# Two-layer mLSTM and retention trunk: head 1's first z column under the gate chain, a reordered start, masks made ahead, the state's low part on VectorE

## The chip, the cores and the metric

The kernel runs on one core of one Trainium2 chip. The metric is the device time of one execution in microseconds (us), as the median of several executions. The engines are named as in the profile: PE is TensorE, DVE is VectorE, ACT is ScalarE, POOL is GpSimd, and SP is the engine whose queue issues all DMA transfers here.

## The reference

Two layers run one after the other on x (1024 tokens by 1024 channels, float32). Each layer does this:

```python
ada = silu(c) @ w_ada[l] + b_ada[l]            # 3072 values: shift, scale, gate
h = rmsnorm(x, norm_g[l]) * (1 + scale) + shift
p = h @ w_in[l]                                # 9224 columns, split among the heads
# 4 mLSTM heads of 256: q and k through a causal convolution over 4 tokens and SiLU; v; o; z;
#   one input and one forget gate value per token and head; a stabilised chunked recurrence
y_m = sigmoid(o) * layernorm(cell) * silu(z)
# 4 retention heads of 256: q and k turned by rotary angles, v, z; decay gamma_h per token
y_r = layernorm(ret) * silu(z)
x = x + gate * (concat(y_m, y_r) @ w_out[l])
```

A last RMSNorm follows the second layer. Everything is float32, and the result is held to float32 accuracy.

## The kernel before

**Products.** A float32 product is made of three fast ones: each operand is split into a high part (a cast on ACT, to the fp32r type) and a low part (the difference, a tensor_tensor on DVE or POOL, in `split_to`), and `mm3` issues high by high, high by low and low by high (lines 134 to 136). The normalised input stands transposed in `hT`, 8 blocks of 128 channels by 2 halves of 512 tokens, each with both parts.

**Units and ticks.** PE's instructions stand in the order in which the program emits them. The projection of 128 columns of `w_in` is four units (`proj_units`): two halves of the tokens, each half in two units of 12 products. After every unit comes a tick. Side work is written as generators that are launched with a delay: at each tick those that are due run to their next yield, and what they emit stands at that place in PE's order. The instructions of the other engines are ordered by a scheduler within their dependences; each engine then runs its own list strictly in order, and so does SP's queue, which carries every DMA.

**The start (layer 0).** A script of short steps orders the work by hand: T transposes a block of x on PE, E scales and shifts it, C and U make its two parts, F multiplies it into the first three weight columns, A adds up rows of `w_ada` on DVE, P and G make scale and shift of two blocks from such a sum, W splits weights, N, Q, R and X normalise rows. `w_ada` is loaded in quarters (`ada_load`), x in halves (`load_x`). DMA transfers of the start are issued in program order: x's first half, the small rows, the first `w_ada` quarter, three weight blocks, the second quarter, and so on.

**The gate chain.** `v0_units` makes head 0's v and the gate values of all heads. `gate_chain` turns the gate values into running sums and maxima per token (scans on DVE, 4 partitions by 512), stores the maxima to DRAM (`mdr`), and 15 ticks after its launch PE transposes its tables (line 492). In layer 0 these ticks are the units of head 0's o column (4), its q columns (8) and 3 units of its k columns.

**Heads.** For each head 0 to 7: gate columns z and o (`gate_path`, z alone for retention heads), q and k (with the convolution on DVE for mLSTM heads, lines 613 to 621), v, then `attention` is launched and runs under the next head's projections. It works on 4 chunks of 256 tokens: `scores` (products of k and q, times a mask), `values` (scores by v, plus the state by q), `update` (the state, in `cf`, split into `cH` by ACT and `cL` by POOL), `finish` (to DRAM). An mLSTM head's mask `dm` is made in `scores`: two transfers from `mdr`, two affine_selects on POOL, two exponentials on ACT. There are two `dm` buffers, and the scheduler already places the mask work of a later chunk, or of the next head, as soon as a buffer is free.

**Other side work in layer 0.** `rotary_tables` is launched after head 1 and computes the angles on DVE. `ada_columns_later` is launched after head 2: it reads layer 1's `w_ada` rows through the four `raw` buffers that the weights use too, and adds them up on DVE (line 255). `gate_rows` is launched after head 5 and does the same for the output gate.

Of the kernel before, what the change touches and what calls it, by code (L numbers as in the profile page):

```python
# [69 lines left out]
def tile_hybrid_trunk(ctx, tc, x, c, positions, w_ada, b_ada, norm_g, w_in, conv_w, conv_b,  # L70
# [285 lines left out]
    def rotary_tables():  # L356
        c1, c2, c3 = two_pi_split()
        tiles = [wt("g", 512, 6) for _ in range(3)]
        ang, turn, tmp, rnd, a1, pos = (t[:, i * CH:(i + 1) * CH] for t in tiles for i in range(2))
        a2 = ang  # L360
        for n in range(4):
            i, cs = n // 2, slice((n % 2) * CH, (n % 2 + 1) * CH)
            Q.dma_start(pos.bitcast(I32), positions[0:1, n * CH:(n + 1) * CH].to_broadcast([P, CH]))
            yield 2
            V.tensor_copy(ang, pos.bitcast(I32))
            V.tensor_scalar(ang, ang, kc[:, C_FREQ:C_FREQ + 1], None, ALU.mult)
            V.tensor_copy(a1.bitcast(F32R), ang)
            yield 1
            V.tensor_tensor(a2, ang, a1, ALU.subtract)
            V.tensor_scalar(turn, a1, c3, None, ALU.mult)  # L370
            yield 1
            V.scalar_tensor_tensor(turn, a2, c3, turn, ALU.mult, ALU.add)
            V.scalar_tensor_tensor(turn, a2, c2, turn, ALU.mult, ALU.add)
            yield 1
            for src, cc in ((a1, c2), (a2, c1), (a1, c1)):
                V.tensor_scalar(tmp, src, cc, None, ALU.mult)
                V.tensor_scalar(rnd, tmp, MAG_I, -MAG_I, ALU.add, ALU.add)
                yield 1
                V.tensor_tensor(tmp, tmp, rnd, ALU.subtract)
                V.tensor_tensor(turn, turn, tmp, ALU.add)  # L380
                yield 1
            for which, sh in ((1, 0.0), (0, 0.25)):
                if sh:
                    V.tensor_scalar(turn, turn, sh, None, ALU.add)
                V.tensor_scalar(rnd, turn, MAG_I, -MAG_I, ALU.add, ALU.add)
                V.tensor_tensor(tmp, turn, rnd, ALU.subtract)
                yield 1
                V.tensor_scalar(tmp, tmp, 0.49999994, -0.49999994, ALU.min, ALU.max)
                Q.dma_start(rdr[which][i][:, cs], tmp)
                yield 2  # L390

    def v0_gates(l):
        gr = wt("wgr", KT * 8, 1)
# [151 lines left out]
    def ocol(hg, m):  # L545
        return OFF_MO + hg * HD + m * P

    def gate_path(l, hg, hT, res, m0=0, m1=2):
        for m in range(m0, m1):
            w = load_w(w_in[l], zcol(hg, m), P)  # L550
            yield from proj_units(w, hT, z_evac(res, m, None if hg < 4 else gdr[l][hg]))
            if hg < 4:
                w = load_w(w_in[l], ocol(hg, m), P)
                yield from proj_units(w, hT, o_evac(res, m, gdr[l][hg]))
# [165 lines left out]
    def attention(l, hg, gt, qT, kT, kt, vs, gp, rot):  # L720
# [3 lines left out]
        nrm = [None] * NCH  # L724
        st = {"state": None, "cf": None}

        def scores(j):
            half, jo = j // 2, (j % 2) * CH
            if ml:
                dm = wt("dm", 512, 2)[:, 0:384]  # L730
                Q.dma_start(dm[:, 0:256], mdr[l][h:h + 1, j * CH:(j + 1) * CH].to_broadcast([P, CH]))
                Q.dma_start(dm[:, 256:384], mdr[l][h:h + 1, j * CH + P:(j + 1) * CH].to_broadcast([P, P]))
                G.affine_select(dm[:, 0:256], dm[:, 0:256], [[1, 256]], ALU.is_ge, BIG, base=0, channel_multiplier=-1)
                G.affine_select(dm[:, 256:384], dm[:, 256:384], [[1, 128]], ALU.is_ge, BIG, base=0, channel_multiplier=-1)
                for tt, sl in ((0, slice(0, 256)), (1, slice(256, 384))):
                    A.activation(dm[:, sl], dm[:, sl], AF.Exp, scale=-1.0, bias=gt["C4"][:, 2 * j + tt, 0, h:h + 1])
                dmat = dm
            else:
                dmat = rmask
            ps = ps_a()  # L740
            pd = ps[:, CH:2 * CH].rearrange("p (a b) -> p a b", a=2)
            for dt in range(2):
                kk, qq = kT[dt][half], qT[dt][j]
                ks = slice(jo, jo + P)
                mm3(ps[:, 0:CH], (kk[0][:, ks], kk[1][:, ks]), (qq[:, 0:CH], qq[:, CH:2 * CH]), dt == 0, dt == 1)
            for dt in range(2):
                kk = kT[dt][half]
                qd = qT[dt][j].rearrange("p (a b) -> p a b", a=2)[:, :, P:CH]
                for i in range(2):
                    PE.matmul(pd, kk[i][:, jo + P:jo + CH], qd, start=dt == 0 and i == 0, stop=dt == 1 and i == 1)  # L750
            sd = wt("th", 512, 5)
            V.tensor_tensor(sd[:, 0:CH], ps[:, 0:CH], dmat[:, 0:CH], ALU.mult)
            V.tensor_tensor(sd[:, CH:2 * CH].rearrange("p (a b) -> p a b", a=2), pd,
                            dmat[:, CH:CH + P].unsqueeze(1).to_broadcast([P, 2, P]), ALU.mult)
            V.tensor_tensor(sd[:, CH:CH + P], sd[:, CH:CH + P], sd[:, CH + P:2 * CH], ALU.add)
            sd = sd[:, 0:CH + P]
            sH, sL = wt("sH", 384, 2, F32R), wt("sL", 384, 2, F32R)
            split_to((sH, sL), sd)
            sds[j] = (sH, sL)

        def update(j):
            if j == 0:
# [4 lines left out]
            for dt in range(2):  # L767
# [7 lines left out]
                else:  # L775
                    dec = gt["dc"][:, h, j - 1:j] if ml else float(np.float32(GAMMA[h] ** CH))
                    V.scalar_tensor_tensor(cf[:, dt, 0:W], cf[:, dt, 0:W], dec, pu[:, 0:W], ALU.mult, ALU.add)
            split_to((new[0][:, :, 0:W], new[1][:, :, 0:W]), cf[:, :, 0:W])
            st["state"] = new

        def values(j):
# [59 lines left out]
        def finish(j):  # L841
# [10 lines left out]
            if hg == 3 and j == NCH - 1:  # L852
                with tc.issue_after(last.ins):
                    load_rotary(rot)

        scores(0)
        yield 1
        scores(1)
        yield 2 if hg == 0 else 1
        for j in range(NCH):  # L860
            values(j)
            yield 1
            if j < NCH - 1:
                update(j)
            yield 1
            if j + 2 < NCH:
                scores(j + 2)
            if hg != 3:
                yield 1
            finish(j)  # L870
            yield 1
# [146 lines left out]
    xss = [new_ss(), new_ss()]  # L1018
    crow = wt("rows", P, 2)
    Q.dma_start(crow[0:8, :], c[0].rearrange("(r c) -> r c", c=P))  # L1020
    xts = [load_x(0)]
    arows = load_ada_rows(0)
    araw = [ada_load(0, 0)]
    firsts = (zcol(0, 0), ocol(0, 0), zcol(0, 1))
    rw = [[w_raw(col, 0)] for col in firsts]
    araw.append(ada_load(0, 1))
# [7 lines left out]
    hrows = load_head_rows(0)  # L1034

    load_cact(crow)
    squares(xts[0], xss[0], range(4), (1, 3))
    accs = [bt()]
    ada_cols(0, arows)
    rs0 = row_rstd(xss[0], "nrm")  # L1040
    ada_group(araw[0], accs[0], range(3))
    norm_scale(xts[0], rs0, (0,), (0, 2))
    ada_group(araw[0], accs[0], range(3, 8))
    pad = ps_a()

    for l in range(DEPTH):
# [14 lines left out]
        if l == 0:  # L1061
            seq = [(half, k) for half in range(2) for k in range(4)]
            seq += [(half, k) for g in (2, 3) for half in range(2) for k in (2 * g, 2 * g + 1)]
            w0, pts, hfs, rs1 = [], {}, {}, []
            script = ("T0 P0 T1 W00 W10 N G0 E0 C0 E1 C1 A102 U0 U1 W20 F0 F1 T2 A126 Q04 A168 P1 G1 E2 C2 R X0 T3 E3 C3 "
# [4 lines left out]
            for step in script.split():  # L1070
# [2 lines left out]
                if what == "T":  # L1073
                    pts[n] = norm_transpose(xts[seq[n][0]], seq[n][1])
                elif what == "E":
                    hfs[n] = norm_evac(0, pts.pop(n), seq[n][1], True)
                elif what == "C":
                    half, k = seq[n]
                    hT[k][half] = (bt(F32R), bt(F32R))
# [16 lines left out]
                    squares(xts[1], xss[1], range(int(arg[0]), int(arg[1])))  # L1096
                elif what == "R":
                    rs1 = row_rstd(xss[1], "nrm")
                elif what == "N":
                    norm_scale(xts[0], rs0, (1,), range(4))  # L1100
                elif what == "X":
                    if n == 0:
                        norm_scale(xts[1], rs1, (0,))
# [5 lines left out]
                        vrw.append(v0_raw(0, n + 4))  # L1109
                else:  # L1110
                    i, p = (int(d) for d in arg)
                    wf[i] += split_w(rw[i][p], P, V)
            head_cols(0, hrows)
            startup.__exit__(None, None, None)
        else:
# [18 lines left out]
        else:  # L1134
            run_units(proj_units(load_w(w_in[l], zcol(0, 1), P), hT, z_evac(gp, 1)))
        run_units(proj_units(load_w(w_in[l], ocol(0, 1), P), hT, o_evac(gp, 1, gdr[l][0])))
        gb = []
        for hg in range(8):
            ml = hg < 4
            if hg == 0:  # L1140
                rot = [[], []]
            if hg > 0:
                gp = [[None, None], [None, None]]
                run_units(gate_path(l, hg, hT, gp, 0, 1 if hg == 7 else 2))
            vs = []
            kt = [None] * NCH
            kT = [[None, None], [None, None]]
# [3 lines left out]
            for which, res in ((0, qT), (1, kT)):  # L1151
                if ml:
                    run_units(qk_ml(l, hg, which, hT, gt, kt, res))
                else:
                    run_units(qk_ret(l, hg % 4, which, hT, kt, res, *rot))
            if hg not in (0, 4):
                run_units(v_path(l, hg, hT, gt, vs))
            if hg == 0:
                launch(v0_splits(gt, vraw, vs), 1)
            launch(attention(l, hg, gt, qT, kT, kt, vs, gp, rot), 4 if hg == 0 else 0)  # L1160
            if hg == 7:
                loads = OutLoads(l)
                loads.stage(2)
# [3 lines left out]
                launch(rotary_tables(), 0)  # L1167
            if hg == 5:
                launch(gate_rows(l, gb))
            if hg == 2 and l + 1 < DEPTH:  # L1170
                launch(ada_columns_later(l + 1))
        nhT = [[None, None] for _ in range(KT)]
        if l == DEPTH - 1:
# [50 lines left out]
```

## Time and profile before

| what | value |
| --- | --- |
| median of 3 executions | 2345.45 us (2345.41 to 2346.18) |
| the profiled execution's own time | 2349.28 us |
| its span, first to last instruction | 2347.6 us |
| mean granted TensorE clock | 0.994 |
| PE busy | 2297.6 us, 98% of the span |
| DVE, ACT, POOL busy | 1283.7, 895.4, 883.8 us |

A window row gives the length of a stretch, then busy us (and number of instructions) of PE, its weight loads, DVE, ACT and POOL, then the granted clock, the share of the DMA engines and GB/s. A wait row gives who waited for whom, total us, how often, and the longest. A timeline row gives start, duration, engine, line, operation, tiles, and in brackets the idle time before it and what ended it. A group row gives busy us, mean ns of one, and the idle time before.

### The profile page before, as it was taken

How to read it: one execution, taken by the hardware profiler on the slowest of the kernel's cores; microseconds unless marked ns; L12 is line 12 of the kernel's file. 1: busy time of each engine (PE TensorE's matmuls, PEld its weight loads, DVE VectorE, ACT ScalarE, POOL GpSimd, SP SyncE). 2: the span in 40 equal slices, each digit the busy share in tenths (PEclk: the TensorE clock that was granted, in tenths of full speed). 3: DMA queues.
4: the chain of work that ended last, by engine and by line, in shares of the span. 5: the costliest groups of instructions: out<-in, count | busy, mean ns of one | idle time of the engine just before them, and what ended most of it. 6: DMA issues, size and time to landing. Idle time of an engine off the chain costs nothing.

```text
span 2347.6 us, 34389 instructions
## 1 busy us (share of the span) xinstructions
PE 2297.6 (98%) x12589; PEld 1980.6 (84%) x12589; DVE 1283.7 (55%) x2694; ACT 895.4 (38%) x1744; POOL 883.8 (38%) x846
## 2 busy tenths in 40 slices
PE   6989999999999999999999999999999999999998
PEld 4878888889988988988888888888898888988886
DVE  7375587655554544475525655455543445456753
ACT  6535343434332323343434444343433322324442
POOL 0344343433344334323453444343333434451313
PEclk9999999999999999999999999999999999999999
DMA  8323232433432424377422323323323323424872
GB/s 253 79 68 86 73 88 72 114 95 105 135 91 72 121 69 113 86 242 255 167 80 76 83 72 78 80 68 81 81 71 81 81 78 103 134 76 157 265 229 81
DMA packets 326970, 260.50 MB, mean 111 GB/s; under 512 B 75892, under 2 KB 262012, under 8 KB 326800
## 3 DMA queue, kind: packets, MB, share of 16 engines
q1 hardware_dynamic: 326800, 258.30, 38.9%
q8 instruction: 99, 1.62, 0.3%
q14 instruction: 71, 0.58, 0.1%
HBM read 202.61 MB, written 55.61 MB: 110 GB/s over the span
## 4 chain that ended last, share of the span: by engine, by line
PE 88%; DVE 4%; DMA 3%; issue 2%; POOL 1%; ACT 1%; SPq 1%; POOLq 0%; ACTq 0%; DVEq 0%
PE pp L134 23%; PE pp L135 23%; PE pp L136 23%; PE pa L136 6%; PE pa L135 6%; PE pa L134 6%; PE pa L750 1%; DMA b<-in_w_ada_dram 1%; DMA b<-in_x_dram 0%; DVE acc L616 0%; POOL b L599 0%; DMA g<-gdr 0%; DMA dm<-mdr 0%; PE pa L304 0%; DMA raw<-in_w_in_dram 0%
## 5 line engine op out<-in xcount | busy, mean ns | idle before, releaser
L134 PE MATMUL pp<-b,wH 128*128 128x512 f32 x1776 | 704.9, 397 | 1.3 <-ACT b L1080 1.3
L135 PE MATMUL pp<-b,wH 128*128 128x512 f32 x1776 | 702.2, 395 | 0.0
L136 PE MATMUL pp<-b,wL 128*128 128x512 f32 x1776 | 702.0, 395 | 0.0
L599 POOL TENSOR_TENSOR wL<-raw,wH 128x512 fp32r<-128x512 f32 x338 | 449.0, 1335 | 582.3 <-ACT wH L598 518.3
L136 PEld LDWEIGHTS pp<-b,wL 128*128 128x128 f32 x1776 | 334.9, 189 | 79.3
L134 PEld LDWEIGHTS pp<-b,wH 128*128 128x128 f32 x1776 | 335.6, 189 | 72.1 <-ACT b L1080 1.7
L135 PEld LDWEIGHTS pp<-b,wH 128*128 128x128 f32 x1776 | 335.3, 189 | 71.2 <-DVE b L1083 0.6
L598 ACT CAST wH<-raw 128x512 fp32r<-128x512 f32 x402 | 247.0, 617 | 377.0 <-PE pp L136 124.8
L136 PE MATMUL pp<-wH,b 128*128 128x256 f32 (+1 forms) x1152 | 353.0, 306 | 2.5 <-DVE b L894 2.5
L134 PE MATMUL pp<-wH,b 128*128 128x256 f32 (+1 forms) x1152 | 353.3, 307 | 0.0
L135 PE MATMUL pp<-wL,b 128*128 128x256 f32 (+1 forms) x1152 | 352.9, 306 | 0.0
L599 POOL TENSOR_TENSOR b<-acc,b 128x256 fp32r<-128x256 f32 (+1 forms) x208 | 200.4, 983 | 316.4 <-ACT b L598 305.1
L136 PEld LDWEIGHTS pp<-wH,b 128*128 128x128 f32 x1152 | 216.7, 188 | 14.7 <-DVE b L894 3.4
L135 PEld LDWEIGHTS pp<-wL,b 128*128 128x128 f32 x1152 | 216.9, 188 | 10.6
L134 PEld LDWEIGHTS pp<-wH,b 128*128 128x128 f32 x1152 | 216.6, 188 | 10.6
L598 ACT CAST b<-acc 128x256 fp32r<-128x256 f32 (+1 forms) x208 | 93.6, 487 | 198.2 <-DVE acc L693 135.8
L616 DVE SCALAR_TENSOR_TENSOR acc<-pp,cols,acc 128x511 f32<-128x511 f32 (+2 forms) x192 | 142.5, 742 | 47.3 <-ACT acc L611 45.2
L599 POOL TENSOR_TENSOR sL<-th,sH 128x384 fp32r<-128x384 f32 x64 | 70.6, 1103 | 154.5 <-ACT sH L598 127.4
L134 PE MATMUL pa<-wH,b 128*128 128x512 f32 x256 | 101.0, 395 | 0.0
L135 PE MATMUL pa<-wL,b 128*128 128x512 f32 x256 | 100.8, 394 | 0.0
L136 PE MATMUL pa<-wH,b 128*128 128x512 f32 x256 | 100.7, 393 | 0.0
L620 ACT ACTIVATE th<-acc 128x512 f32<-128x512 f32 x64 | 40.4, 632 | 149.8 <-DVE acc L618 77.2
(249 smaller groups left out, 3485.1 us busy)
## 6 DMA issues: line engine op xcount, KB each, us to landing
raw<-in_w_in_dram SPq DMA_DIRECT2D x274, 256.0 KB
raw<-in_w_out_dram SPq DMA_DIRECT2D x128, 256.0 KB
gdr<-g SPq DMA_DIRECT2D x64, 256.0 KB
ndr<-zt SPq DMA_DIRECT2D x128, 128.0 KB
raw<-in_w_ada_dram SPq DMA_DIRECT2D x64, 256.0 KB
g<-ndr SPq DMA_DIRECT2D x64, 256.0 KB
g<-gdr SPq DMA_DIRECT2D x64, 256.0 KB
acc<-kdr SPq DMA_DIRECT2D x192, 64.0 KB
```

The lines of the kernel that those rows point to most:

```text
L134: PE.matmul(o, lt[0], rt[0], start=start, stop=False)
L135: PE.matmul(o, lt[0], rt[1], start=False, stop=False)
L136: PE.matmul(o, lt[1], rt[0], start=False, stop=stop)
L598: A.copy(dst[0], src)
L599: eng.tensor_tensor(dst[1], src, f(dst[0]), ALU.subtract)
L616: V.scalar_tensor_tensor(acc[:, d:], pt[:, 0:HALF - d], wcol, acc[:, d:], ALU.mult, ALU.add)
L620: A.activation(th, acc, AF.Tanh, scale=0.5)
L750: PE.matmul(pd, kk[i][:, jo + P:jo + CH], qd, start=dt == 0 and i == 0, stop=dt == 1 and i == 1)
```

## The change

1. **z column.** In layer 0 the projection of head 1's first z column (`zcol(1, 0)`) is emitted right after head 0's last o column, so that its four units stand among the 15 ticks before the gate chain's transposes. Head 1's `gate_path` leaves it out.
2. **Start.** The first `w_ada` quarter is loaded ahead of x's first half. Its sum is made first, then x is squared and normalised (new steps S and N0 in the script). The first two blocks are scaled on DVE instead of ACT, and the low parts of the first three weight blocks move from DVE to POOL.
3. **Masks.** `scores` is divided: `dm_load` issues the transfers (the first two at the start of `attention`, the later ones at the end of `scores(j)` for chunk j+2) and `dm_make` the affine_selects and exponentials (for chunk j+2 after `values(j)`). For heads 1 to 3 `attention` is launched before the v projection with a delay of 7, and head 0's delay falls from 4 to 2, so that the scores stand at the tick at which they stood.
4. **State.** The state's low part `cL` is made on DVE instead of POOL, for all heads of both layers.
5. **Side work.** `ada_columns_later` is launched after head 3 instead of head 2. `rotary_tables` writes its sine and cosine into two buffers and issues both transfers together.

```diff
-            for which, sh in ((1, 0.0), (0, 0.25)):
+            parts = ((1, 0.0, tmp), (0, 0.25, a1))
+            for which, sh, dst in parts:
...
+            for which, sh, dst in parts:
+                Q.dma_start(rdr[which][i][:, cs], dst)
+            yield 2
...
-    def gate_path(l, hg, hT, res, m0=0, m1=2):
+    def gate_path(l, hg, hT, res, m0=0, m1=2, z0=True):
...
+            if m or z0:
+                w = load_w(w_in[l], zcol(hg, m), P)
...
+        def dm_load(j):
+            if ml and j < NCH:
+                dm = dms[j] = wt("dm", 512, 2)[:, 0:384]
...
+        def dm_make(j):
+            if ml and j < NCH:
+                dm = dms[j]
...
             split_to((sH, sL), sd)
             sds[j] = (sH, sL)
+            dm_load(j + 2)
...
-            split_to((new[0][:, :, 0:W], new[1][:, :, 0:W]), cf[:, :, 0:W])
+            split_to((new[0][:, :, 0:W], new[1][:, :, 0:W]), cf[:, :, 0:W], V)
...
+        if ml:
+            dm_load(0)
+            dm_load(1)
+            yield 1
+            dm_make(0)
+            dm_make(1)
+            yield 1
         scores(0)
...
             values(j)
             yield 1
+            dm_make(j + 2)
...
-    xts = [load_x(0)]
     arows = load_ada_rows(0)
     araw = [ada_load(0, 0)]
+    xts = [load_x(0)]
...
-    squares(xts[0], xss[0], range(4), (1, 3))
+    ada_cols(0, arows)
     accs = [bt()]
-    ada_cols(0, arows)
-    rs0 = row_rstd(xss[0], "nrm")
-    ada_group(araw[0], accs[0], range(3))
-    norm_scale(xts[0], rs0, (0,), (0, 2))
-    ada_group(araw[0], accs[0], range(3, 8))
+    ada_group(araw[0], accs[0], range(KT))
...
-            script = ("T0 P0 T1 W00 W10 N G0 E0 C0 E1 C1 A102 U0 U1 W20 F0 F1 T2 A126 Q04 A168 P1 G1 E2 C2 R X0 T3 E3 C3 "
+            script = ("P0 G0 S N0 T0 T1 W00 W10 E0 E1 C0 C1 U0 U1 W20 F0 F1 N1 T2 A103 Q04 A136 A168 P1 G1 E2 C2 R X0 T3 E3 C3 "
...
-                    hfs[n] = norm_evac(0, pts.pop(n), seq[n][1], True)
+                    hfs[n] = norm_evac(0, pts.pop(n), seq[n][1], n >= 2)
...
-                    wf[i] += split_w(rw[i][p], P, V)
+                    wf[i] += split_w(rw[i][p], P, V if p else G)
...
+        gp1 = [[None, None], [None, None]]
+        if l == 0:
+            run_units(proj_units(load_w(w_in[l], zcol(1, 0), P), hT, z_evac(gp1, 0)))
...
+            if 0 < hg < 4:
+                launch(attention(l, hg, gt, qT, kT, kt, vs, gp, rot), 7)
...
-            launch(attention(l, hg, gt, qT, kT, kt, vs, gp, rot), 4 if hg == 0 else 0)
+            if hg == 0 or hg > 3:
+                launch(attention(l, hg, gt, qT, kT, kt, vs, gp, rot), 2 if hg == 0 else 0)
...
-            if hg == 2 and l + 1 < DEPTH:
+            if hg == 3 and l + 1 < DEPTH:
                 launch(ada_columns_later(l + 1))
```

More of the change, by code (lines that the diff above doesn't have):

```diff
@@ L385, in rotary_tables @@
                 V.tensor_scalar(rnd, turn, MAG_I, -MAG_I, ALU.add, ALU.add)
-                V.tensor_tensor(tmp, turn, rnd, ALU.subtract)
+                V.tensor_tensor(dst, turn, rnd, ALU.subtract)
                 yield 1
-                V.tensor_scalar(tmp, tmp, 0.49999994, -0.49999994, ALU.min, ALU.max)
-                Q.dma_start(rdr[which][i][:, cs], tmp)
-                yield 2
+                V.tensor_scalar(dst, dst, 0.49999994, -0.49999994, ALU.min, ALU.max)
+            yield 2
+            for which, sh, dst in parts:
+                Q.dma_start(rdr[which][i][:, cs], dst)
+            yield 2
     def v0_gates(l):
@@ L546, in ocol @@
         return OFF_MO + hg * HD + m * P
-    def gate_path(l, hg, hT, res, m0=0, m1=2):
+    def gate_path(l, hg, hT, res, m0=0, m1=2, z0=True):
         for m in range(m0, m1):
-            w = load_w(w_in[l], zcol(hg, m), P)
-            yield from proj_units(w, hT, z_evac(res, m, None if hg < 4 else gdr[l][hg]))
+            if m or z0:
+                w = load_w(w_in[l], zcol(hg, m), P)
+                yield from proj_units(w, hT, z_evac(res, m, None if hg < 4 else gdr[l][hg]))
             if hg < 4:
@@ L725, in attention @@
         st = {"state": None, "cf": None}
[L727 to L730, printed above, removed]
+        dms = {}
+        def dm_load(j):
+            if ml and j < NCH:
+                dm = dms[j] = wt("dm", 512, 2)[:, 0:384]
                 Q.dma_start(dm[:, 0:256], mdr[l][h:h + 1, j * CH:(j + 1) * CH].to_broadcast([P, CH]))
                 Q.dma_start(dm[:, 256:384], mdr[l][h:h + 1, j * CH + P:(j + 1) * CH].to_broadcast([P, P]))
+        def dm_make(j):
+            if ml and j < NCH:
+                dm = dms[j]
                 G.affine_select(dm[:, 0:256], dm[:, 0:256], [[1, 256]], ALU.is_ge, BIG, base=0, channel_multiplier=-1)
@@ L736, in scores @@
                     A.activation(dm[:, sl], dm[:, sl], AF.Exp, scale=-1.0, bias=gt["C4"][:, 2 * j + tt, 0, h:h + 1])
-                dmat = dm
-            else:
-                dmat = rmask
+        def scores(j):
+            half, jo = j // 2, (j % 2) * CH
+            dmat = dms.pop(j) if ml else rmask
             ps = ps_a()
@@ L1098, in tile_hybrid_trunk @@
                     rs1 = row_rstd(xss[1], "nrm")
+                elif what == "S":
+                    squares(xts[0], xss[0], range(4), (1, 3))
+                    rs0 = row_rstd(xss[0], "nrm")
                 elif what == "N":
-                    norm_scale(xts[0], rs0, (1,), range(4))
+                    norm_scale(xts[0], rs0, (n,), range(4) if n else (0, 2))
                 elif what == "X":
@@ L1142, in tile_hybrid_trunk @@
             if hg > 0:
-                gp = [[None, None], [None, None]]
-                run_units(gate_path(l, hg, hT, gp, 0, 1 if hg == 7 else 2))
+                gp = gp1 if hg == 1 else [[None, None], [None, None]]
+                run_units(gate_path(l, hg, hT, gp, 0, 1 if hg == 7 else 2, hg > 1 or l > 0))
             vs = []
```

## The prediction

> **What bounds the kernel now.** I read the page's busy shares first, then PE's waits over the whole run, then windows laid around each wait, then the timeline inside them. On the page PE is the bound:
>
> ```profile
> PE 2297.6 (98%) x12589; PEld 1980.6 (84%) x12589; DVE 1283.7 (55%) x2694; ACT 895.4 (38%) x1744; POOL 883.8 (38%) x846
> ```
>
> The change adds and removes no product, so it can win only PE's idle time, 2347.6 - 2297.6 = 50.0 us, and what PE loses at a low clock after a pause. PE's waits, longest totals of interest, with count and longest:
>
> ```profile
> PE pa L492 <- DVE b L482: 7.0, 1, 7.0
> ...
> PE pa L134 <- ACT nd L796: 4.9, 2, 3.4
> ...
> PE pa L135 <- POOL cL L599: 1.6, 2, 1.2
> ...
> PE pa L136 <- POOL sL L599: 1.3, 2, 0.6
> ```
>
> The windows around them: length, then busy us of PE, its loads, DVE, ACT, POOL, and the granted clock.
>
> ```profile
> 98.40:141.20 42.80, 42.79 (x187) 34.45 (x186) 34.52 (x50) 21.32 (x32) 14.71 (x15) 1.00 0.25 60
> 141.20:148.20 7.00, 0.00 (x0) 0.00 (x0) 6.81 (x12) 2.02 (x4) 2.32 (x2) 0.85 0.05 1
> 148.20:153.00 4.80, 4.76 (x14) 3.91 (x15) 4.77 (x18) 3.72 (x11) 2.69 (x3) 0.50 0.31 37
> ...
> 326.00:329.50 3.50, 1.40 (x9) 0.82 (x7) 2.92 (x7) 2.83 (x7) 1.58 (x2) 1.00 0.32 115
> ...
> 354.80:357.50 2.70, 1.25 (x5) 0.57 (x5) 2.70 (x6) 1.62 (x3) 1.66 (x2) 1.00 0.29 84
> ...
> 458.10:464.50 6.40, 2.97 (x15) 2.12 (x13) 0.43 (x2) 1.77 (x5) 1.07 (x3) 0.93 0.58 168
> 464.50:470.00 5.50, 5.50 (x19) 4.93 (x20) 3.25 (x15) 1.68 (x4) 1.59 (x2) 0.50 0.19 48
> 560.00:625.00 65.00, 63.93 (x444) 59.17 (x443) 36.09 (x107) 24.14 (x53) 23.82 (x23) 1.00 0.34 96
> 1295.00:1480.00 185.00, 184.36 (x998) 158.47 (x997) 107.28 (x258) 86.04 (x178) 78.17 (x81) 1.00 0.31 78
> ```
>
> The reader should see two large holes, at the gate chain (141.2) and under head 3's gate columns (458.1), each followed by a stretch at half clock. The last row is layer 1's first heads, without rotary tables and without `w_ada` rows under them: 0.64 us idle in 185 us. What is lost in layer 0 is therefore lost to side work, which the change moves.
>
> **z column under the gate chain.** PE waits 7.00 us at line 492 and then runs 4.80 us at 0.50 of its clock, which costs another 4.80 x 0.50 = 2.40 us: 9.4 us in all. The Trainium skill, "TensorE: Matmul & The Clock Gate" (What's actually happening), has the array at half rate until one busy window of about 3.4 us has passed, which would be 1.7 us instead of 2.40 and would make the final sum 0.7 us later.
>
> PE reaches the transposes after 15 units in both kernels, so 141.2 stays. What must come earlier is DVE's line 482. Between 122.68, when the first half column of q is through, and 148.10 DVE also did the following convolution work (three answers of the windows view, restricted to lines 616, 618 and 621 in this order), and the gate chain ended behind it:
>
> ```profile
> 122.68:148.10 25.42, 6.55 (x9) 0.96 0.21 50
> 122.68:148.10 25.42, 3.23 (x5) 0.96 0.21 50
> 122.68:148.10 25.42, 1.39 (x3) 0.96 0.21 50
> ...
> 147.41 0.69 DVE L482 TENSOR_TENSOR b<-b,b 4x512 f32<-4x512 f32 x1
> ...
> L528 DVE SCALAR_TENSOR_TENSOR g<-th,pp 128x512 f32<-128x512 f32 x62 | 42.0, 677 | 49.1 <-ACT th L526 49.1
> ```
>
> That is 11.17 us. In the changed order of DVE's instructions only one of these (the first line 616 of the second half column, 6.55 / 9 = 0.73) still stands ahead of the chain's last instruction; two z evacuations at 0.68 come in instead. So the chain ends 11.17 - 0.73 - 1.36 = 9.1 us earlier, at 148.1 - 9.1 = 139.0, against 141.2. The wait goes with 2.2 us to spare, and the half clock with it: -9.4 (bounds -9.4 and -4.7, if half of the work stays ahead). What is late next is head 0's mask and decay tables, which now have four units more before they are needed. The z transfers and the weights of that column pass no queue they did not use before. Head 0's attention, on the other hand, now runs under 12 gate units and then q's convolutions, where it had 16: I take +0.5, between 0 and +1.3, the total of the sL waits quoted above.
>
> **`w_ada` rows moved from head 2 to head 3.** The hole at 458.1:
>
> ```profile
> 452.14 2.78 DVE L255 SCALAR_TENSOR_TENSOR b<-raw,cact,b 128x512 f32<-128x512 f32 x2 [0.62 <-DMA raw<-in_w_ada_dram]
> ...
> 455.18 0.41 DVE L753 TENSOR_TENSOR th<-pa,dm 128x256 f32<-128x256 f32 x1
> ...
> 457.56 0.49 SPq L731 DMA_DIRECT2D dm<-mdr  x1
> ...
> 462.30 0.40 POOL L733 TENSOR_SCALAR_AFFINE_SELECT dm<-dm 128x256 f32<-128x256 f32 x1 [4.37 <-DMA dm<-mdr]
> 462.73 0.80 ACT L736 ACTIVATE dm<-dm,COL 128x256 f32<-128x256 f32 x2 [5.47 <-POOL dm L733]
> ...
> 463.94 0.83 ACT L796 ACTIVATE nd<-pa,wd 128x258 f32<-128x258 f32 x2
> ```
>
> DVE adds up two rows (2.78 us) before it uses head 2's mask at 455.18; only then is the buffer free, SP issues head 3's mask behind queued rows and weights (457.56), and ACT, in order, stands 5.47 us at that mask's exponential while the `nd` copy behind it keeps PE's bank. The price is 6.40 - 2.97 = 3.43 idle plus 5.50 x 0.50 = 2.75 at half clock, 6.2 us. Making masks ahead does not cure this: in ACT's changed list head 3's first exponential still stands ahead of that `nd`. What cures it is that no `w_ada` rows lie there any more. I take -5.9, bounds -6.2 and 0.
>
> The rows now start under head 3's attention, where 65.00 - 63.93 = 1.07 us is lost today. Head 4 is a retention head and has no mask in ACT's list to stand at, so I take +0.5, bounds -1.1 and +6.2. Further on they run under heads 4 to 6 and overlap `gate_rows`; I cost that at nothing, covered by weights split ahead of their use, and if that cover is gone it is inside the same +6.2.
>
> **State's low part on DVE, masks, rotary.** The prices: POOL's two shapes, a DVE operation of the same kind and nearly the same size, and one DVE shape beside and without POOL's work (the first ran while POOL made `cL`).
>
> ```profile
> L599 POOL TENSOR_TENSOR cL<-cf,cH 128x516 fp32r<-128x516 f32 x24 | 31.9, 1331 | 28.4 <-ACT cH L598 28.4
> L599 POOL TENSOR_TENSOR cL<-cf,cH 128x512 fp32r<-128x512 f32 x24 | 31.6, 1316 | 41.3 <-ACT cH L598 41.3
> ...
> L599 DVE TENSOR_TENSOR wL<-raw,wH 128x512 fp32r<-128x512 f32 x64 | 50.0, 794 | 38.4 <-ACT wH L598 38.2
> ...
> 316.70 1.41 DVE L379 TENSOR_TENSOR g<-g 128x256 f32<-128x256 f32 x1
> ...
> 319.34 0.42 DVE L379 TENSOR_TENSOR g<-g 128x256 f32<-128x256 f32 x1
> ```
>
> The step gets 1.33 - 0.79 = 0.54 us shorter. It is on the path only at 354.8 (1.45 us idle, the cL wait) and once under head 3, so all else is hidden under PE. At 326.0 (2.10 us idle) ACT stands at head 2's mask as above, and the order there is unchanged; the DVE work ahead of it loses a POOL neighbour (0.42 against 1.41). For both I take -1.5 of 3.55 (bounds 0 and -3.6). "GPSIMD Engine Reference" (1. Specifications) of the Trainium skill speaks against the move: GpSimd shares its SBUF interfaces with VectorE and contends with DVE instructions of two SBUF inputs, as `cL` is; stretched like L379 it would take about 2.7 us, the -1.5 would become an estimated +1.3, and the sum would be 2.8 later.
>
> **The start.** The transfers ahead of the first product are the same number, in another order.
>
> ```profile
> 1.66 3.67 SPq L999 DMA_DIRECT2D b<-in_x_dram  x8
> ...
> 7.53 4.79 SPq L225 DMA_DIRECT2D b<-in_w_ada_dram  x8
> ...
> 11.00 0.69 DVE L1007 SCALAR_TENSOR_TENSOR th<-b 128x512 f32<-128x512 f32 x1
> ...
> 12.41 1.19 POOL L951 TENSOR_TENSOR rs<-s,mhalf 128x4 f32<-128x4 f32 x1 [9.91 <-DVE s L950]
> ...
> 19.18 2.56 ACT L297 ACTIVATE b<-b,rs 128x512 f32<-128x512 f32 x4
> ...
> 23.11 0.80 PE L134 MATMUL pp<-b,wH 128*128 128x512 f32 x1 [1.33 <-ACT b L1080]
> ...
> 26.05 0.63 ACT L1010 ACTIVATE th<-b 128x512 f32<-128x512 f32 x1 [1.15 <-DMA b<-in_x_dram]
> ```
>
> x's last square started 11.00 - 5.33 = 5.67 us after its last issue; issued at 12.32 instead it starts at 17.3 to 18.0. To the end of the power it is 13.60 - 11.00 = 2.6 us, and scaling, transposing, evacuating and casting take an estimated 3.0 (some four steps at the 0.64 of an ACT operation, and waits): first product at 22.9 to 23.6, against 23.11. The squares of x's second half then wait behind one cast, one weight cast and four scalings on ACT, 23.25 + 0.62 + 0.62 + 2.56 = 27.0 against 26.05, and PE stands for the rows that they normalise before the third block. I take +1.0, bounds 0 and +2. The low parts moved to POOL lie in its empty start.
>
> **Sum.** -9.4 + 0.5 - 5.9 + 0.5 - 1.5 + 1.0 = -14.8. The profiled execution took 2349.28, 3.83 above the median of the runs; 2349.28 - 14.8 - 3.83 = 2330.6.
>
> **Rivals.** (a) The collision of rows and attention moves to head 3 whole: 5.7 later, 2336.3. For it: the same raw buffers, the same queue. Against: no next mask there. 0.16. (b) Half of the gate wait stays, 2335.3: for it, DVE is busy 6.81 of 7.00 us in that wait. 0.07. (c) The mask part does what it says only on paper and head 2's hole stays without any rows: 2336.5. Head 1's hole, without rows, speaks for it; layer 1's 0.64 us against. 0.07. (d) Slower: DVE, in order, stands at each of the 48 `cL` until ACT has made `cH`, as POOL does today (28.4 + 41.3 = 69.7 us), and evacuations queue behind it. If PE pays only the 0.79 us of each, that is 48 x 0.79 = 37.9, so 2368.5; it decides the sign from 0.31 us each (14.8 / 48), and slower by over 0.2% from 0.41. Against it: DVE is idle 45% of the run, and the state has two to three units until its use. 0.08. (e) Better: head 1's holes go whole, 2328.5. 0.09. Two or three of (a) to (c) together reach about 2341 to 2347: 0.05.
>
> **How the numbers follow.** The forecast keeps 0.48. Within 0.2% (4.7 us) is about what this kernel's measurement cannot tell from no change. Faster: 0.48 + 0.16 + 0.07 + 0.07 + 0.09 = 0.87; same 0.05; slower 0.08. The range runs from 2324 (case (e) with an unchanged start and head 3's 1.07 gone too, rounded down) to 2341 ((a) with (b)), leaving out (d) and most of the joint case.
>
> **What would show it.** Right: no wait at the gate transposes and clock 1.00 behind them; no hole between heads 2 and 3; a hole of about 2 us left under head 1; first product near 23, third block one us later. Wrong: new PE waits on `cL` from DVE, a hole under head 3 at the `nd` copies, or weights late where the rows and `gate_rows` overlap.

## The result, and the profile after

The changed kernel takes 2335.65 us in the median of five executions (2333.22 to 2336.09), beside 2345.45 (2343.87 to 2347.28) for the kernel before: a ratio of 0.9955, interval 0.994 to 0.9969. It is 9.8 us faster where 14.8 were forecast. Its profiled execution took 2335.92 us, 0.27 above its median, with a span of 2334.2 and a mean clock of 0.998.

The page's busy shares of the changed kernel:

```profile
PE 2291.8 (98%) x12589; PEld 1975.1 (85%) x12589; DVE 1303.6 (56%) x2741; ACT 892.1 (38%) x1742; POOL 824.4 (35%) x801
```

PE is still the bound. It is idle for 2334.2 - 2291.8 = 42.4 us where it was idle for 50.0. Of the gain of 13.4 us in the two spans, 7.6 is less idle time, and 5.8 is shorter busy time for the same 12589 products (2297.6 to 2291.8), which fits the half clock that is gone (before their last 10 us, the first profile has 20.5 us at half clock and this one 6.8). PE's waits:

```profile
PE pa L240 <- DVE b L235: 10.3, 2, 9.3
PE pa L304 <- ACT b L297: 5.4, 1, 5.4
PE pa L135 <- DVE cL L603: 3.1, 2, 2.8
...
PE pa L136 <- POOL sL L603: 1.5, 3, 0.6
PE pa L134 <- ACT cH L602: 1.1, 1, 1.1
PE pa L134 <- ACT n L849: 1.0, 1, 1.0
```

The wait at the gate transposes (now line 495) is gone from the list, and `nd`, 4.9 us before, is down to 0.5 for ACT's copies. New is a wait of 2.8 us for `cL` from DVE. The largest waits, in both kernels, are those of the start. In the kernel before:

```profile
PE pa L186 <- DMA rows<-in_b_ada_dram: 8.4, 1, 8.4
...
PE pa L240 <- DVE b L235: 3.8, 2, 3.2
...
PE pa L304 <- ACT b L297: 2.6, 1, 2.6
```

The wait at line 186 falls to 0.6 us and the other two grow, so that the three together are 1.5 us longer with the new start. Windows of the changed kernel, laid around the places shown before (columns as there: length, PE, loads, DVE, ACT, POOL, clock, DMA, GB/s):

```profile
139.50:146.50 7.00, 7.00 (x36) 5.80 (x35) 5.00 (x17) 4.23 (x12) 2.69 (x3) 1.00 0.10 1
146.50:151.30 4.80, 4.80 (x23) 3.88 (x22) 3.12 (x8) 2.52 (x7) 2.77 (x3) 1.00 0.21 54
...
344.20:347.50 3.30, 1.90 (x12) 1.27 (x11) 3.30 (x10) 2.22 (x5) 0.60 (x1) 1.00 0.32 79
450.00:470.00 20.00, 20.00 (x115) 17.48 (x114) 9.60 (x34) 7.78 (x16) 5.72 (x7) 1.00 0.38 90
571.50:576.50 5.00, 2.22 (x11) 1.72 (x10) 4.64 (x7) 1.00 (x2) 3.00 (x2) 0.85 0.64 192
576.50:581.50 5.00, 5.00 (x27) 4.56 (x27) 4.19 (x15) 1.85 (x4) 1.09 (x2) 0.81 0.68 200
```

The gate chain and head 2 run without a hole and at clock 1.00. Head 1 keeps a small hole (344.2). Head 3 has a new one, 2.78 us idle, with the clock down in it and behind it. Its timeline:

```profile
567.78 1.24 DVE L841 TENSOR_TENSOR rsd<-rsd,qd 128x2 f32<-128x2 f32 x1 [3.48 <-POOL rsd L840]
...
571.08 0.71 DVE L255 SCALAR_TENSOR_TENSOR b<-raw,cact,b 128x512 f32<-128x512 f32 x1
...
571.58 3.00 POOL L603 TENSOR_TENSOR wL<-raw,wH 128x512 fp32r<-128x512 f32 x2 [2.58 <-issue]
...
572.14 1.32 DVE L255 SCALAR_TENSOR_TENSOR b<-raw,cact,b 128x512 f32<-128x512 f32 x1 [0.36 <-DVE b L255]
573.39 1.75 DVE L603 TENSOR_TENSOR cL<-cf,cH 128x516 fp32r<-128x516 f32 x1
...
575.20 0.58 PE L135 MATMUL pa<-cL,b 128*128 128x258 f32 x1 [2.78 <-DVE cL L603]
```

`cL` stands behind two sums of `w_ada` rows in DVE's list. The second sum and `cL` run beside two weight splits on POOL and take 1.32 and 1.75 us; in the mean this shape of `cL` takes 0.79:

```profile
L603 DVE TENSOR_TENSOR cL<-cf,cH 128x512 fp32r<-128x512 f32 x24 | 19.7, 822 | 11.9 <-ACT cH L602 11.9
L603 DVE TENSOR_TENSOR cL<-cf,cH 128x516 fp32r<-128x516 f32 x24 | 19.0, 790 | 12.5 <-ACT cH L602 12.5
```

To see where the time came from, the start of the same product in PE's list was compared in both traces, at places where the orders coincide. The lag of the changed kernel against the one before goes +0.4 (at 75 us), -9.1 (276), -10.8 (413), -16.6 (503), -13.0 (933), -13.4 (the end).

### The profile page after: what moved, and what is told of

The parts are those of the page before. It is cut to its first block, busy times and chain, and to the rows that moved or that the text cites. A ratio compares the mean times of both kernels' runs of the same rounds, so it can differ in the third digit from the quotient of the medians.

```text
span 2334.2 us, 34424 instructions
## 1 busy us (share of the span) xinstructions
PE 2291.8 (98%) x12589; PEld 1975.1 (85%) x12589; DVE 1303.6 (56%) x2741; ACT 892.1 (38%) x1742; POOL 824.4 (35%) x801
## 5 line engine op out<-in xcount | busy, mean ns | idle before, releaser
L134 PEld LDWEIGHTS pp<-wH,b 128*128 128x128 f32 x1152 | 216.7, 188 | 10.8
L135 PEld LDWEIGHTS pp<-wL,b 128*128 128x128 f32 x1152 | 216.7, 188 | 10.7
```

Source lines behind the costliest of these rows:

```text
L134: PE.matmul(o, lt[0], rt[0], start=start, stop=False)
L135: PE.matmul(o, lt[0], rt[1], start=False, stop=False)
```

## The experiments

Each ratio is to the kernel before on the same chip.

**The z column alone** (edit 1 on the kernel before).

```diff
...
+        if l == 0:
+            run_units(proj_units(load_w(w_in[l], zcol(1, 0), P), hT, z_evac(gp1, 0)))
...
```

> The kernel before with the first part alone: head 1's first z column under the gate chain. Theory: the gate wait (7.0 us) and the half clock behind it (2.4 us) go whole, nothing comes instead; no wait at the gate transposes, clock 1.00 behind them, span 9.4 us shorter (9.7 is what the two traces show at this place), head 2's hole at 458 stays; time about 2336. Rival: most of the changed kernel's gain is other parts and half of the wait stays, 4.7 us, time about 2340.7. Rival: the wait only moves to head 0's attention, which has four units less ahead of it; then a new wait of several us stands there and the time stays within 2 us of 2345.

2336.82 us, ratio 0.9959 (0.9946 to 0.9971): 9.8 us by the medians. No wait for the gate chain is left among PE's waits. This one edit gives as much as the whole change.

**The rows alone** (one line on the kernel before).

```diff
-            if hg == 2 and l + 1 < DEPTH:
+            if hg == 3 and l + 1 < DEPTH:
                 launch(ada_columns_later(l + 1))
```

> The kernel before with one line changed: the rows of the second layer's conditioning are launched after head 3 instead of after head 2; masks, state and start as before. Theory: the rows are the cause of head 2's hole, so it goes without any change of the masks (5.7 us less up to 550 us), and heads 3 to 6 give back what the rows cost there. If that price comes from the state's low part on VectorE behind the rows, no wait for it shows here and the give-back is about 0.5 us: time about 2340. If the price belongs to the rows wherever they stand, 3.5 us come back: time about 2343. Rival: the masks made ahead cured the hole; then it stays and the time is 2345 or more.

2343.56 us, ratio 0.9988 (0.9979 to 0.9997): 3.0 us. Head 2's hole is gone with the masks as they were, so the rows were its cause:

```profile
452.00:476.00 24.00, 24.00 (x136) 20.94 (x135) 10.18 (x34) 8.80 (x18) 8.95 (x11) 1.00 0.38 91
```

At head 3 a wait for `cL` appears, and here POOL makes it:

```profile
PE pa L135 <- POOL cL L599: 2.9, 2, 2.2
```

**The state's low part back on POOL** in the changed kernel.

```diff
-            split_to((new[0][:, :, 0:W], new[1][:, :, 0:W]), cf[:, :, 0:W], V)
+            split_to((new[0][:, :, 0:W], new[1][:, :, 0:W]), cf[:, :, 0:W])
```

> The changed kernel with the state's low part back on GpSimd, all else as changed. Theory: the wait of 2.8 us at head 3 (572 us) is the low part queued on VectorE behind two row sums, so it goes or falls under 1 us; head 1's holes grow by up to 1.5 us. Sum: 1 to 2 us faster than the changed kernel, about 2334. Rival 1: GpSimd, with two weight splits ahead of it there (3.00 us for two), makes the low part as late, the wait stays under another name, and head 1 loses: 2336 to 2337. Rival 2: VectorE is worth what the 48 steps are shorter (48 x 0.54 = 26 us): 2350 or more.

2340.78 us, ratio 0.9974 (0.9964 to 0.9984), slower, not faster: the theory falls, and rival 1 has what happens, with too small a price. The wait at head 3 stays whichever engine makes `cL`:

```profile
PE pa L135 <- POOL cL L603: 3.3, 2, 2.2
```

What was lost lies at head 1: 5.2 us of lag come there, some 1.7 of them at a lower clock behind its holes:

```profile
344.50:350.00 5.50, 3.75 (x17) 2.72 (x15) 3.10 (x13) 2.86 (x6) 2.11 (x3) 1.00 0.23 58
350.00:355.50 5.50, 4.27 (x20) 4.07 (x21) 5.26 (x10) 2.10 (x5) 2.71 (x2) 0.69 0.01 3
```

**The kernel before, once more.**

> The kernel before once more, unchanged, for one more profile. Theory: the profiled execution of 2349.28 us lay 3.8 us above its median because of one execution's accident, so this one comes within 1.5 us of 2345.5 and the difference from the first profile can be found at one or two places. Rival: profiling itself makes this kernel's executions 3 to 4 us longer; then this one is near 2349 again, and the changed kernel's profile, only 0.3 us above its median, would be the odd one.

2343.17 us, 6.1 below the first profile and 2.3 below the kernel's median of 2345.45. The rival falls: a profiled execution need not be long. In 18 other executions on this chip it took from 2343.14 to 2350.05, median 2346.59, so neither profile is out of the ordinary. Of the 6.1, 1.7 lie at the start (6.83 us at half clock from 33.53 in the first profile, 3.41 from 33.80 in this one), 0.8 at the gate chain and 2.6 at head 2; the rest is spread over the run behind it. At head 2 the first execution idled and then had 0.50 of its clock for 5.50 us; this one idled as long (wait row 3.5 us against 3.4) and kept 1.00:

```profile
455.80:462.20 6.40, 2.91 (x14) 2.05 (x12) 0.39 (x2) 1.72 (x5) 0.98 (x3) 1.00 0.60 170
462.20:467.70 5.50, 5.49 (x34) 4.96 (x35) 3.25 (x15) 1.68 (x4) 1.66 (x2) 1.00 0.20 48
```

**The changed kernel, once more,** on the chip of the next three.

> The changed kernel once more, unchanged, on the chip of the next three, so that they can be set against it. Theory: 2334 to 2336, a ratio near 0.9955, and the same places in its profile: no hole at the gate chain or under head 2, one wait of 2 to 3 us near 572 us. Rival: where the kernel before differed by 6 us between two profiles, this one does too, and the single wait at 572 us is one execution's accident.

2336.14 us, ratio 0.9958 (0.9944 to 0.9972). The wait for `cL` is there again, 2.8 us long, so it belongs to the kernel. Behind it PE had 6.83 us at half clock here, 3.41 in the first profile.

**The masks as before** in the changed kernel.

```diff
-        dms = {}
...
+                dm = wt("dm", 512, 2)[:, 0:384]
...
+            launch(attention(l, hg, gt, qT, kT, kt, vs, gp, rot), 4 if hg == 0 else 0)
```

> The changed kernel with the masks made inside the scores and the attention launched where it was in the kernel before; all else as changed. Theory: with z column alone at 9.8 us, rows alone at 3.0 us and the state's low part at 5 us in the changed kernel, the parts add up to 18 us where 9.8 were measured, so another part costs several us; head 1's holes were larger with the low part on GpSimd in the changed kernel (9.2 us lost from 300 to 375 us) than in the kernel before (5.6 us), and the masks are the part that touches that place. Then this kernel is 2 to 5 us faster than the changed one: 2331 to 2334. Rival: the masks gain what they were meant to gain, and it is 2 us or more slower: 2338 or more. Rival: they change nothing that can be seen, within 1 us, and the rotary transfers issued together are what costs.

2337.5 us, ratio 0.9958 (0.9945 to 0.997), the same as the changed kernel. The theory's gain is not there, and of the first rival's loss of 2 us nothing shows, though intervals of this width could hide it: the mask edit does nothing that can be measured.

**The start as before** in the changed kernel.

```diff
...
-            script = ("P0 G0 S N0 T0 T1 W00 W10 E0 E1 C0 C1 U0 U1 W20 F0 F1 N1 T2 A103 Q04 A136 A168 P1 G1 E2 C2 R X0 T3 E3 C3 "
+            script = ("T0 P0 T1 W00 W10 N G0 E0 C0 E1 C1 A102 U0 U1 W20 F0 F1 T2 A126 Q04 A168 P1 G1 E2 C2 R X0 T3 E3 C3 "
...
```

> The changed kernel with the start of the kernel before (x loaded first, squares first, first two blocks scaled on ScalarE, low parts on VectorE). Theory: the start costs the forecast 1.0 us, 0.5 by the two first profiles and 1.3 to 2.2 against the other profiles of the old start: this kernel is 0.5 to 2 us faster, 2334. Rival: the new start pays, and it is 1 us or more slower. The place to read is PE's lag at 75 us, before anything else differs.

2333.94 us, ratio 0.9947 (0.9935 to 0.996), 2.2 below the changed kernel, with intervals that overlap. The traces are clearer: the 251st product in PE's list starts at 73.26 to 75.14 us in the eight profiles with the old start (mean 74.3) and at 75.32 to 76.68 in the six with the new one (mean 76.0). The new start costs 1.7 us.

**The rows one head later** in the changed kernel.

```diff
-            if hg == 3 and l + 1 < DEPTH:
+            if hg == 4 and l + 1 < DEPTH:
```

> The changed kernel with the conditioning rows launched one head later still, after head 4. Theory: the wait of 2.8 us at 572 us came with the rows whether VectorE or GpSimd makes the low part (2.2 us in the kernel before with the rows moved), so it goes, and the rows then meet retention heads without masks; but they overlap with the output gate's rows more: +0 to 2 us there. Sum: 1 to 3 us faster, about 2333. Rival: the price moves on with the rows to head 4's attention, whole: 2336. Rival: the overlap delays weights, and the time is 2338 or more.

2331.1 us, ratio 0.9934 (0.9921 to 0.9946), 5.0 below the changed kernel. Two windows of the same stretch, the changed kernel's and then this one's:

```profile
560.00:625.00 65.00, 62.22 (x418) 57.65 (x417) 37.33 (x96) 27.31 (x54) 21.03 (x21) 0.97 0.43 125
```

```profile
560.00:625.00 65.00, 65.00 (x438) 59.90 (x437) 28.65 (x88) 27.59 (x55) 19.62 (x21) 1.00 0.33 88
```

PE has no idle time left at head 3, and VectorE does 8.7 us less there. Under the retention heads the rows cost a wait of about 1 us near 800 us, as they do near 788 in the changed kernel.

**Two edits only,** z column and rows after head 4, on the kernel before.

```diff
...
+            run_units(proj_units(load_w(w_in[l], zcol(1, 0), P), hT, z_evac(gp1, 0)))
...
-            if hg == 2 and l + 1 < DEPTH:
+            if hg == 4 and l + 1 < DEPTH:
...
```

> The kernel before with two edits only: the z column under the gate chain, and the conditioning rows after head 4; start, masks, rotary and state as before. Theory: z is worth 9.8 us and the rows after head 3 3.0 us by themselves, one head later 4.5 us more, so 17 us: about 2329.5, a ratio near 0.9927, as fast as the changed kernel with the same move of the rows (2331.1). Rival: the state's low part on VectorE is worth the 5 us at head 1 that the changed kernel lost without it; then this is 2334 or more.

2329.0 us, ratio 0.9927 (0.9914 to 0.9941), as expected. It beats both kernels, without any of the other edits.

**The changed kernel with rows after head 4 and the old start.**

> The changed kernel with the rows after head 4 and the start of the kernel before: the two edits that made the changed kernel faster, together. Theory: they lie 500 us apart and add up, 4.5 and 1.3 us (by the lag at 75 us): about 2329.8. Rival: the shift of 1.3 us at the start is eaten by the next wait at head 1, and the time stays at 2331.

2328.08 us (2327.71 to 2330.47), ratio 0.9927 (0.9915 to 0.994). It cannot be told from the two-edit kernel: masks, rotary and the state's low part add nothing that can be measured to it.

**The state's low part on VectorE, alone,** on the kernel before.

> The kernel before with the state's low part on VectorE, nothing else. Theory: the step is shorter by 0.54 us and on the path at two places only (head 1, head 3), so 1 to 2 us come, 2345 against 2346.5. Rival: it is worth the 5 us that the changed kernel lost when the step went back to GpSimd: 2341.5. Rival: VectorE stands at each of the 48 steps and it is slower, 2350 or more.

2343.77 us, ratio 0.9991 (0.9982 to 1.0): some 2 us, and the interval reaches no change. By the trace 1.2 us come at head 1. Rival (d) of the prediction is out: PE does not pay at each of the 48 steps. In this run head 2's pause was only 2.3 us by its wait row, and the clock fell all the same:

```profile
457.20:460.20 3.00, 0.71 (x4) 0.28 (x2) 0.12 (x1) 1.83 (x5) 1.13 (x3) 1.00 0.20 75
460.20:465.70 5.50, 5.50 (x23) 4.85 (x24) 3.25 (x15) 1.68 (x4) 1.55 (x2) 0.69 0.19 48
```

**The rotary tables as before** in the changed kernel.

```diff
-            parts = ((1, 0.0, tmp), (0, 0.25, a1))
...
+            for which, sh in ((1, 0.0), (0, 0.25)):
...
```

> The changed kernel with the rotary tables as in the kernel before (one temporary, each transfer issued as soon as its half is made). By themselves the z column (9.8), the rows (3.0) and the state's low part (5 in the changed kernel) come to 18 us, the start takes 1 to 2 and the masks nothing, and 10 to 11 us were measured: 5 us are missing. Theory: the low part is worth so much only in the changed kernel because its rotary tables, with 2 more ticks for each part, press harder on VectorE under head 1; then this kernel is 1 to 4 us faster, 2332 to 2335, with smaller holes from 330 to 350 us. Rival: the rotary edit costs nothing, 2336, and the 5 us are another order of VectorE's list that the state's step brings.

2334.55 us, ratio 0.9953 (0.994 to 0.9965), beside 0.9958: not to be told apart. The holes from 330 to 350 us are no smaller, 2.1 us of idle time against 2.0 and 2.5 in the changed kernel's two profiles, so nothing speaks for the theory. Why the low part is worth more in the changed kernel (some 4 us by the ratios, 5.2 by the traces) than in the one before (2) stays open in part. Of the 5.2, 1.7 are a piece of half clock behind a hole near 350 us, and the same piece stands there, from 347 us, in three profiles that have the low part on VectorE (the old start, the rows one head later, and both together). The order of VectorE's list differs between the kernels too. Nor do 5 us have to be missing: z column (9.8), rows (3.0), the low part by itself (2) and the new start (-1.7) sum to 13.1, and 9.8 and 10.7 were measured.

## Why the prediction was right or wrong

The direction and the two large terms were right; the forecast of 2330.6 was 5.0 us too low. That splits into two errors: the subtraction of 3.83 us, and 1.4 us in the sum (2349.28 - 14.8 = 2334.5, measured 2335.92), less 0.3 by which the changed kernel's profile lay above its median. Beside the medians of the parts that were run alone, the largest miss is the rows: 5.4 us forecast for leaving head 2 and arriving at head 3 together, 3.0 measured.

- **"2349.28 - 14.8 - 3.83" took some of the time off twice.** The step took the 3.83 us by which the profiled execution exceeded its median as something that stays and can be taken off besides. It did not stay: the changed kernel's profile lay 0.27 above its median. Of the 6.1 us between the two profiles of before, 3.4 lie at places that the change clears (2.6 behind head 2's hole, 0.8 at the gate chain). A hole that was dearer than usual in the profiled run was removed at its full price, and its excess then taken off again. The 1.7 at the start are no such place. They went as well, because the changed kernel's profile has the short piece of half clock there, and they hid what the new start costs. How the 3.83 themselves divide is not known, as no execution at the median was profiled. Half clock was a term of the sum (2.75), and it is also what varies from run to run.
- **z column under the gate chain: right.** The trace has -9.5 by 276 us, with head 0's attention in it, where -9.4 + 0.5 was forecast; alone the edit gives 9.8. Head 0's +0.5 did not come. The chain's last instruction ended earlier still, at 137.33 against 139.0 forecast, and PE came to the transposes at 141.08 as forecast:

```profile
136.31 1.02 DVE L485 TENSOR_TENSOR b<-b,b 4x512 f32<-4x512 f32 x1
...
141.08 1.03 PE L495 MATMUL pa<-ident,b 128*128 128x128 f32 x8
```

- **Rows leave head 2: right,** -5.7 against -5.9, and for the reason given (the rows alone do it; the masks do not). But that is the price of the first profile, and of its clock. From 413 to 503 us the first profile took 6.4 us longer than the run of the rows alone, which has no such hole; the three later profiles with the hole took 3.8, 5.4 and 4.1 us longer.
- **Rows arrive at head 3: mis-sized,** +0.5 forecast, +3.5 in the trace up to 933 us, and +2.9 to +6.1 in the six other profiles with the rows there, inside the bounds of -1.1 and +6.2. The reason, "head 4 is a retention head and has no mask to stand at", looked only at the mechanism of head 2's hole. What the rows meet is head 3's state: `cL` comes late, behind row sums on VectorE or made by GpSimd. Rival (a) had the place right and its time, 2336.3, is near the result, by luck: its 5.7 is the price of a dear execution, and the collision it had in mind was another.
- **State, masks, rotary: right in the first trace, by luck.** There -1.7 came at head 1 against -1.5 forecast. In the four other profiles with the changed kernel's heads 0 to 3, the same stretch (276 to 413 us) was 0.9 us shorter than in the first profile of before, and 0.1, 0.2 and 0.6 longer; the three long ones have 3.41 us at half clock behind head 1's hole. Masks and rotary do nothing that can be measured, as the argument from ACT's list had it for the masks.
- **The start: mis-sized a little,** 1.7 us over fourteen profiles against 1.0; the two first profiles alone show 0.4, because the kernel before happened to have the longer half clock there. x's last square and the first product came as forecast:

```profile
17.27 0.69 DVE L1026 SCALAR_TENSOR_TENSOR th<-b 128x512 f32<-128x512 f32 x1
...
23.21 0.80 PE L134 MATMUL pp<-b,wH 128*128 128x512 f32 x1 [0.70 <-ACT b L1095]
```

- **The contention rule of the Trainium skill** ("GPSIMD Engine Reference", 1. Specifications) would, by the prediction's estimate, have made `cL` 2.7 us each and the sum 2.8 later. The measured means of 0.79 and 0.82 speak against that as a general price. Where the two engines meet, the trace agrees with the rule. Of the 48 `cL` in the changed kernel's profile, 37 met no work of POOL and took 0.69 us in the mean. The seven that began while a weight split ran on POOL all ended 0.54 or 0.55 us after that split, and took 1.00 to 1.78. One of these seven, at 697.95, and one of the 37:

```profile
696.18 2.99 POOL L603 TENSOR_TENSOR wL<-raw,wH 128x512 fp32r<-128x512 f32 x2 [1.84 <-ACT wH L602]
...
697.95 1.77 DVE L603 TENSOR_TENSOR cL<-cf,cH 128x512 fp32r<-128x512 f32 x1
...
1343.35 0.70 DVE L603 TENSOR_TENSOR cL<-cf,cH 128x516 fp32r<-128x516 f32 x1
```

- **The range's lower end.** The terms named for 2324 give 2328.5 - 1.0 - 1.57 = 2325.9, so it was rounded down by 2 us. Nothing else hangs on it.

## What to carry to other kernels

When a sum is made against one profiled execution, ask where that execution lost more than its median before taking the difference off: if it lost it where the change acts, it is in the sum already. Side work that is moved should be followed to everything it meets at the new place, not only to the kind of wait it caused at the old one; one head further would have cost nothing at head 3. And try the parts alone: here two edits of a few lines give 0.9927, the whole change 0.9955. Last, price a short pause by its idle time, and treat the half clock behind it as something that comes in some executions and not in others.

## What the runs showed of the hardware

The same pause does not always cost the clock. Head 2's hole left 0.50, 1.00 and 0.69 of the clock in the 5.50 us behind waits of 3.4, 3.5 and 2.3 us. The traces' record of the granted clock shows what differs. In all fourteen profiles each piece of half clock, but for the one that the end of the run cuts off, is 3.41 or 6.83 us long, and the places where the clock changes lie whole multiples of 3.413 us apart: in the first profile it falls at 33.53, 146.17 and 463.61 us, 33 and then 93 times 3.413 later. So the run can be cut into cells of 3.41 us. Windows laid on these cells around head 2's hole, in the first profile of the kernel before, in its second, and with the state's low part alone on VectorE:

```profile
460.19:463.61 3.42, 0.85 (x4) 0.37 (x2) 0.00 (x0) 0.88 (x3) 0.69 (x2) 1.00 0.46 116
463.61:467.02 3.41, 2.55 (x12) 2.56 (x13) 2.37 (x10) 1.16 (x3) 1.27 (x1) 0.50 0.11 17
467.02:470.43 3.41, 3.41 (x10) 2.74 (x10) 1.36 (x6) 1.84 (x4) 0.70 (x1) 0.50 0.20 60
```

```profile
457.06:460.47 3.41, 1.65 (x8) 1.01 (x6) 0.00 (x0) 0.00 (x0) 0.42 (x2) 1.00 0.74 190
460.47:463.88 3.41, 1.67 (x13) 1.67 (x14) 1.58 (x5) 2.05 (x5) 1.51 (x2) 1.00 0.00 1
463.88:467.30 3.42, 3.42 (x20) 2.89 (x19) 1.45 (x10) 0.95 (x2) 0.70 (x1) 1.00 0.32 77
```

```profile
457.33:460.74 3.41, 1.12 (x8) 0.69 (x7) 0.62 (x2) 2.04 (x5) 1.67 (x3) 1.00 0.17 61
460.74:464.15 3.41, 3.41 (x14) 3.03 (x14) 2.35 (x13) 0.00 (x0) 1.01 (x2) 0.50 0.30 77
464.15:467.57 3.42, 3.42 (x21) 3.01 (x20) 2.12 (x5) 2.13 (x5) 1.17 (x1) 1.00 0.16 32
```

In the first profile the hole leaves a cell with PE busy for 25%. The next is at half clock and still partly idle, 75% busy, and the one after it is at half clock too. In the second an equally long hole is shared by two cells, 48% and 49% busy, and nothing follows. In the third the shorter hole lies in one cell, 33% busy, and one follows. Counted over the fourteen profiles, from 40 us to the last 8: behind each of 18 cells at full clock in which PE was busy for 45% or less, the next was at half clock; of 11 between 48% and 56%, two were followed by one; from 57% up, none. After a cell at half clock a second one came in all seven cases in which PE was busy in it for 75% or less, and none where it was busy for 84% or more. (These shares come from the profile, in which the ends of matmuls are modelled.) So the 7 us at the gate chain left 6.83 us of half clock in all four profiles that have this wait, while waits of 2 to 4 us left 0, 3.41 or 6.83 us, as they fell on the cells.

In the Trainium skill, "TensorE: Matmul & The Clock Gate" (What's actually happening) describes a free-running window of 3413 ns whose place against the work varies from run to run, and the cells agree with that. Its condition of an idle window of about 3.4 us before the clock falls is too strict here: a cell in which PE was busy for up to 45% was enough.
